# Second norm by its weights alone, the row applied to up's results, one more column pair by seven products, and down's first operands loaded earlier

## The chip, the cores and the metric

The kernel runs on one core of one Trainium2 chip. The metric is the device time of one execution in microseconds; of several runs the median is given.

## The reference

Two layers of an encoder work on 1024 prompt frames and 8 x 16 new frames of running streams, 1152 columns in all, with 1024 features. In each layer one input projection feeds three kinds of attention heads, an output projection adds their result to x, and an MLP with 4096 inner features follows. The change lies in the MLP:

```python
def _rmsnorm(x, g):
    x32 = x.astype(f32)
    y = x32 * lax.rsqrt(jnp.mean(x32 * x32, axis=-1, keepdims=True) + EPS)
    return (y * g.astype(f32)).astype(x.dtype)

def _mlp(h, w_up, w_down):
    return jnp.square(jax.nn.relu(h @ w_up)) @ w_down
...
        xp = xp + _merge(o_mla, o_gla, g_out, o_ca, gla_out_norm[l], w_out[l])
        xp = xp + _mlp(_rmsnorm(xp, norm2[l]), w_up[l], w_down[l])
```

Per frame the norm is one factor r = rsqrt(mean(x^2) + eps) times a weight per feature. Since r is positive and the same for all features of a frame, relu(r z)^2 = (relu(z) r)^2, and (relu(z) r)^2 needs r only after the product with w_up.

## The kernel before

Features lie on the 128 partitions, frames along the free axis: x is 8 tiles of 128 x 1152 (`xs`), worked on in three groups of G = 384 columns (`gsl(g)`). All products are done with float32 operands split in a high part, rounded to the format of the matmul, and the low rest; each product is three matmuls (high x high, high x low, low x high). `wsplit` and `w_pair` split weights (copy on ScalarE, subtraction on VectorE), `hpc` gives the tiles for split activations from one tag of 48 buffers in turn, `piece` the passing float32 tiles from a tag of 8.

The order on each engine is not written out: the framework orders instructions by a simulated time line, with the order of the program as priority; `tc.high_priority(offset=...)` lifts a block. All transfers go through one queue, that of SyncE, in that order.

The MLP of a layer runs so:

- **Norm** (`norm_group`, `inv_rms`): for each group, squares and sums of the 8 tiles on ScalarE, VectorE and GpSimd; a matmul with ones sums over partitions (tile `ms`), a few small operations make r (`rr`), and matmuls spread it to all partitions (`rb`). Then for each of the 8 tiles VectorE makes x * weight * r (`hf`), ScalarE the high part (`hH`), and VectorE or GpSimd the low part (`hL`). The row r of groups 0 and 1 is kept in `rs`. x goes to memory as `xmid`.
- **Up**: w_up has 32 column blocks, taken in 16 pairs. `up_plain(i, gs)` multiplies pair i for the groups gs. `up_seven(i, rest)` does groups 0 and 1 of a pair as a 2 x 2 block product (two column blocks, two halves of the features, two groups) with seven products instead of eight; it needs sums and differences of blocks of weights (`ws`, split to `wus`) and of activations (`ts`). With rest true it multiplies group 2 plainly (`third`). The sums of activations are made once per layer by `t_prep(j)`, j = 0..3, which loads x again from `xmid` (tile `f`, 4 buffers), multiplies it with weights and r, and forms four sums, each split in two. Pairs 0, 1 and 2 are plain, pairs 3 to 15 go by seven products, of which 3 to 12 with group 2; group 2 of pairs 13, 14, 15 follows plainly at the end.
- **put_u** turns a result z into u = relu(z)^2 and stores it to memory: ScalarE relu and a GpSimd multiplication, or for two of the results of a seven-product pair one VectorE operation. Its tile `u` has 5 buffers, shared with the loads `ur` below.
- **Down**: 8 blocks b of 4 tiles of u. `load_u(b)` loads the 12 pieces of a block, splits them to `uH` and `uL`, and `down_block` multiplies them with w_down (`wdn`) and adds to x; block 0 takes x from `xmid`.

PSUM is given out by `banks`: 6 banks for results (`d`) and 2 for the norm during the norm and pair 0, then 8 for results. `w_raw` loads a block of weights into one of 2 buffers (`wr`).

Of the kernel before, what the change touches and what calls it, by code (L numbers as in the profile page):

```python
# [9 lines left out]
F32 = mybir.dt.float32  # L10
F32R = mybir.dt.float32r
U32 = mybir.dt.uint32
AF = mybir.ActivationFunctionType
ALU = mybir.AluOpType
AX = mybir.AxisListType

P = 128
# [4 lines left out]
G = 384  # L22
NG = NT // G
KD = 8
# [16 lines left out]
def body(ctx, tc, t):  # L41
# [5 lines left out]
    V, S, T, GP = nc.vector, nc.scalar, nc.tensor, nc.gpsimd  # L47
# [3 lines left out]
    def nm(s):  # L51
        uid[0] += 1
        return f"{s}_{uid[0]}"
# [19 lines left out]
    def load(dst, src):  # L73
        nc.sync.dma_start(dst, src)  # L74
# [4 lines left out]
    def open_pool(stack, s, side="left"):  # L79
        return stack.enter_context(tc.tile_pool(name=nm(s), bufs=1, reuse_waits="tile", side=side))  # L80
# [5 lines left out]
    def hpc(s, dt=F32R):  # L86
        return hpool.tile([P, G], dt, tag="h", name=nm(s), bufs=48)
# [5 lines left out]
    def piece(s, shape=None, dt=F32):  # L93
        return ppool.tile(list(shape) if shape else [P, G], dt, tag="p", name=nm(s))
# [42 lines left out]
    def sub_l(eng, lo, src, h):  # L137
        eng.tensor_tensor(lo, src, h.bitcast(F32), ALU.subtract)  # L138
# [14 lines left out]
    def copy(o, i, scale=1.0):  # L153
        S.activation(o, i, AF.Copy, scale=scale)  # L154

    def gsl(g):
        return slice(g * G, (g + 1) * G)
# [41 lines left out]
    def norm_group(xs, gains, hs, g, pool=SQ_POOL):  # L199
        r = inv_rms([x[:, gsl(g)] for x in xs], 1024.0, pool=pool)  # L200
        for c in range(KD):
            hs[c].append((hpc("hH"), hpc("hL")))
            f = piece("hf")
            V.scalar_tensor_tensor(f, xs[c][:, gsl(g)], gains[:, c:c + 1], r, ALU.mult, ALU.mult)  # L204
            copy(hs[c][g][0], f)
            sub_l(V if c % 2 else GP, hs[c][g][1], f, hs[c][g][0])
        return r

    def new_h():
        return [[] for _ in range(KD)]  # L210
# [15 lines left out]
    xs = [xpool.tile([P, NT], F32, name=nm("x")) for _ in range(KD)]  # L226
# [23 lines left out]
    for l in range(DEPTH):  # L250
# [88 lines left out]
        hs = new_h()  # L339
# [876 lines left out]
        xs = [xpool.tile([P, NT], F32, name=nm("x")) for _ in range(KD)]  # L1216
# [30 lines left out]
        ustack, tstack = ExitStack(), ExitStack()  # L1247
        up = open_pool(ustack, "up")
        wextra[0], wturn[0] = up, 0
        gains = sml[:, SM_N2:SM_N2 + 8]  # L1250
        hs = new_h()
        rs = []
        for g in range(NG):
            with tc.high_priority(offset=100):
                r = norm_group(xs, gains, hs, g)
                if g < 2:
                    rs.append(up.tile([P, G], F32, name=nm("rs")))
                    copy(rs[g], r)
                for c in range(KD):
                    store(t["xmid"][:, c, gsl(g)], xs[c][:, gsl(g)])  # L1260
        xstack.close()
        tpool = open_pool(tstack, "tsum", "right")
        ts = [[] for _ in range(5)]

        def u_tile(s):
            return up.tile([P, G], F32, tag="u", name=nm(s), bufs=5)

        def t_prep(j):
            fs = []
            for c in (j, j + KH):  # L1270
                for g in range(2):
                    f = tpool.tile([P, G], F32, tag="f", name=nm("f"), bufs=4)
                    load(f, t["xmid"][:, c, gsl(g)])
                    V.scalar_tensor_tensor(f, f, gains[:, c:c + 1], rs[g], ALU.mult, ALU.mult)
                    fs.append(f)
            f11, f12, f21, f22 = fs
            t1, t2, t3, t4 = (piece("t") for _ in range(4))
            V.tensor_tensor(t1, f12, f11, ALU.subtract)
            V.tensor_tensor(t2, f22, t1, ALU.subtract)
            V.tensor_tensor(t4, f21, t2, ALU.subtract)  # L1280
            GP.tensor_tensor(t3, f22, f12, ALU.subtract)
            for n, f in ((2, t2), (3, t3), (1, t1), (4, t4)):
                o = tuple(tpool.tile([P, G], F32R, name=nm("ts")) for _ in range(2))
                copy(o[0], f)
                sub_l(V, o[1], f, o[0])
                ts[n].append(o)
# [11 lines left out]
            load(raw, src)  # L1298
            return raw

        def put_u(ci, g, z, eng):

            u = u_tile("u")
            if eng is None:
                V.scalar_tensor_tensor(u, z, 0.0, z, ALU.max, ALU.mult)
            else:
                r = piece("r")
                S.activation(r, z, AF.Relu)  # L1308
                eng.tensor_tensor(u, r, r, ALU.mult)  # L1309
            store(t["u"][l, ci, :, gsl(g)], u)  # L1310

        def up_plain(i, gs):
            w = [w_pair(w_raw(t["w_up"][l, 2 * i + c]), "wup") for c in range(2)]
            for g in gs:
                for c in range(2):
                    o = bank("d", "z")[:, :G]
                    dense(o, w[c], lambda k: hs[k][g], KD)
                    put_u(2 * i + c, g, o, GP)

        def up_seven(i, rest):  # L1320
            raw = [w_raw(t["w_up"][l, 2 * i + c]) for c in range(2)]
            a11, a12, a21, a22 = (raw[x][:, y * KH:(y + 1) * KH, :] for x in range(2) for y in range(2))
            sa, sb = (tpool.tile([P, KD, P], F32, tag="ws", name=nm("ws"), bufs=2) for _ in range(2))
            s2, s3, s1, s4 = sa[:, :KH], sa[:, KH:], sb[:, :KH], sb[:, KH:]
            GP.tensor_tensor(s1, a21, a22, ALU.add)
            GP.tensor_tensor(s3, a11, a21, ALU.subtract)
            V.tensor_tensor(s2, s1, a11, ALU.subtract)
            V.tensor_tensor(s4, a12, s2, ALU.subtract)

            def prod(o, w, half, x, first):  # L1330
                for j in range(KH):
                    for k, (wi, ri) in enumerate(((0, 0), (0, 1), (1, 0))):
                        mm(o, w[wi][:, half * KH + j, :], x[j][ri], start=first and j == k == 0,
                           stop=j == KH - 1 and k == 2, skip_group_check=True)

            def third(w, c):
                if rest:
                    o = bank("d", "z")[:, :G]
                    dense(o, w, lambda k: hs[k][2], KD)
                    put_u(2 * i + c, 2, o, GP)  # L1340

            def add(s, o, e):
                z = piece(s)
                V.tensor_tensor(z, o, e, ALU.add)
                return z

            h1 = [[hs[j][g] for j in range(KH)] for g in range(2)]
            h2 = [[hs[j + KH][g] for j in range(KH)] for g in range(2)]
            X, Y, W, Z = (bank("d", "z")[:, :G] for _ in range(4))
            w = w_pair(raw[0], "wup")  # L1350
            prod(X, w, 0, h1[0], True)
            ea = ppool.tile([P, G], F32, tag="q", name=nm("ea"), bufs=4)
            copy(ea, X)
            third(w, 0)
            prod(X, w, 1, h2[0], False)
            put_u(2 * i, 0, X, GP)
            w = w_pair(sa, "wus")
            prod(Y, w, 0, ts[2], True)
            eb = add("eb", Y, ea)
            prod(W, w, 1, ts[3], True)  # L1360
            ec = add("ec", W, eb)
            ws = w_pair(sb, "wus")
            prod(Z, ws, 0, ts[1], True)
            put_u(2 * i + 1, 1, add("z22", Z, ec), None)
            w = w_pair(raw[1], "wup")
            third(w, 1)
            prod(W, w, 1, ts[4], False)
            put_u(2 * i + 1, 0, add("z21", W, eb), None)
            prod(Z, ws, 1, h2[1], False)
            put_u(2 * i, 1, add("z12", Z, eb), GP)  # L1370

        up_plain(0, range(NG))
        banks(d=8)
# [2 lines left out]
        up_plain(1, range(NG))  # L1376
        t_prep(2)
        t_prep(3)
        up_plain(2, range(NG))
        for i in range(3, 16):  # L1380
            up_seven(i, i < 13)
        for i in range(13, 16):
            up_plain(i, (2,))
        tstack.close()


# [1 line left out]
        xpool = open_pool(xstack, "x", "right")  # L1388
        xs = [xpool.tile([P, NT], F32, name=nm("x")) for _ in range(KD)]

        def load_u(b):
            us = []
            for q in range(4):
                row = []
                for g in range(NG):
                    r = u_tile("ur")
                    load(r, t["u"][l, 4 * b + q, :, gsl(g)])
                    o = hpc("uH"), hpc("uL")
                    copy(o[0], r)
                    sub_l(V, o[1], r, o[0])  # L1400
                    row.append(o)
                us.append(row)
            return us

        def down_block(us, b, gs):
            for m in range(KD):
# [12 lines left out]
                    V.tensor_tensor(x, o, x if xo is None else xo, ALU.add)  # L1419

        for b in range(8):
            us = load_u(b)
            if b == 7:
                banks(d=6, nm=2)
            for gs in ((range(NG),) if b < 7 else ((0,), (1,), (2,))):
                down_block(us, b, gs)
# [134 lines left out]
```

## Time and profile before

| | us |
|---|---|
| median of 3 runs | 3238.74 |
| lowest, highest run | 3233.21, 3239.31 |
| profiled execution, its own time | 3230.82 |
| its span, first to last instruction | 3229.0 |
| mean granted TensorE clock | 0.976 of full |
| busy: TensorE, VectorE, ScalarE, GpSimd | 3053.8, 1947.0, 1319.7, 987.2 |
| MLP of layer 0, from the last output projection to its end | about 790 to 1600 |
| MLP of layer 1 | about 2390 to 3210 |

Engines in the profile: PE is TensorE's matmul, PEld its weight load, DVE VectorE, ACT ScalarE, POOL GpSimd, SPq the queue of SyncE that issues transfers. A line of a group or of a tile names the line of the code (often a helper's: L56 is every matmul, L138 every subtraction of a high part, L154 every copy), the tiles as out<-in, sizes and count. In a timeline the first two numbers are start and length in us, and in brackets stands how long the engine was idle before and what ended that. A granted clock of 1.00 is full speed.

### The profile page before, as it was taken

The page shows a single profiled execution, that of the slowest core. Times are in us where ns is not written, and L with a number is a line of the kernel's source. Part 1 is how long each engine was busy: PE and PEld are TensorE (multiplying, and loading weights), DVE is VectorE, ACT ScalarE, POOL GpSimd, SP SyncE. Part 2 cuts the span into 40 slices and gives each one's busy share as a digit, 9 for nine tenths or more (in the row PEclk, how much of TensorE's full clock was granted, in tenths as well). Part 3 has the DMA queues.
Part 4 walks back from the last instruction along what each step waited for, and adds up shares of the span by engine and source line. Part 5 has one row for each costly group of instructions (what it writes and reads, how often), then busy time and mean ns, then how long its engine had stood idle before and what let it go on. Part 6 is the DMA issues. An engine that isn't in the chain of part 4 may idle for free.

```text
span 3229.0 us, 50225 instructions
## 1 busy us (share of the span) xinstructions
PE 3053.8 (95%) x18196; PEld 2920.9 (90%) x18196; DVE 1947.0 (60%) x3805; ACT 1319.7 (41%) x2907; POOL 987.2 (31%) x1170
## 2 busy tenths in 40 slices
PE   7999998998999989999999999988999999899998
PEld 7888887887999989999989898878889999899998
DVE  4665597885844555444556646968857444554446
ACT  4554454774322232212345534557743222322213
POOL 4332356552533320000143313655534233200002
PEclk9999999999999999999999999999999999999999
DMA  5333215225322345322343322142353222543223
GB/s 178 113 100 102 91 50 163 77 81 180 117 96 93 102 154 182 99 71 90 115 149 121 101 82 86 63 145 78 109 168 105 97 99 98 183 144 98 92 70 118
DMA packets 221719, 360.20 MB, mean 112 GB/s; under 512 B 27136, under 2 KB 185568, under 8 KB 221472
## 3 DMA queue, kind: packets, MB, share of 16 engines
q1 hardware_dynamic: 221472, 357.00, 34.5%
q8 instruction: 144, 2.36, 0.3%
q14 instruction: 103, 0.84, 0.1%
HBM read 253.87 MB, written 103.02 MB: 111 GB/s over the span
## 4 chain that ended last, share of the span: by engine, by line
PE 74%; DVE 12%; ACT 5%; DMA 4%; issue 3%; POOL 1%; SPq 1%; DVEq 0%; ACTq 0%; POOLq 0%
PE z L56 62%; PE pv L56 3%; PE s L56 2%; PE ptp L71 2%; DMA wr<-in_w_up_dram 1%; DVE hf L204 1%; SPq L74 1%; ACT P L419 1%; DMA cf<-zs_dram 1%; PE glao L56 1%; DVE ng L414 1%; PE rb L56 1%; DVE sbd L825 1%; DVE mq L763 1%; DVE ga L772 1%
## 5 line engine op out<-in xcount | busy, mean ns | idle before, releaser
L56 PE MATMUL z<-uH,wdn 128*128 128x384 f32 x3072 | 786.4, 336 | 10.3 <-ACT uH L154 10.3
L56 PEld LDWEIGHTS z<-uH,wdn 128*128 128x128 f32 x3072 | 558.2, 189 | 11.5 <-ACT uH L154 11.5
L56 PE MATMUL z<-uL,wdn 128*128 128x384 f32 x1536 | 515.0, 336 | 0.0
L56 PE MATMUL z<-hH,wup 128*128 128x384 f32 x1824 | 472.9, 334 | 1.0 <-ACT r L1308 1.0
L1419 DVE TENSOR_TENSOR x<-z,x 128x384 f32<-128x384 f32 x336 | 186.7, 556 | 311.7 <-PE z L56 310.6
L56 PEld LDWEIGHTS z<-hH,wup 128*128 128x128 f32 x1824 | 330.2, 188 | 1.6 <-ACT r L1308 1.6
L56 PE MATMUL z<-hL,wup 128*128 128x384 f32 x912 | 306.6, 336 | 8.5 <-DVE hL L138 7.8
L56 PEld LDWEIGHTS z<-uL,wdn 128*128 128x128 f32 x1536 | 290.0, 189 | 0.0
L1309 POOL TENSOR_TENSOR u<-r 128x384 f32<-128x384 f32 x140 | 163.5, 1172 | 373.7 <-ACT r L1308 263.5
L169 POOL TENSOR_TENSOR sq<-x 128x384 f32<-128x384 f32 x28 | 26.4, 944 | 813.5 <-DVE x L1419 742.0
L1292 ACT ACTIVATE wdn<-wr 128x1024 fp32r<-128x1024 f32 x80 | 84.7, 1059 | 461.0 <-PE z L56 459.9
L138 DVE TENSOR_TENSOR wup<-wr,wup 128x1024 fp32r<-128x1024 f32 x76 | 96.4, 1268 | 203.4 <-ACT wup L1292 203.2
L419 ACT ACTIVATE P<-s,ng 128x320 f32<-128x320 f32 (+5 forms) x288 | 157.7, 552 | 96.4 <-DVE ng L416 61.9
L56 PEld LDWEIGHTS z<-hL,wup 128*128 128x128 f32 x912 | 171.2, 188 | 12.1 <-DVE hL L138 10.8
L56 PE MATMUL z<-ts,wus 128*128 128x384 f32 x936 | 171.7, 340 | 6.5 <-ACT wus L1292 5.9
L138 DVE TENSOR_TENSOR PT<-ptp,PT 128x512 fp32r<-128x512 f32 (+3 forms) x288 | 146.4, 515 | 51.7 <-ACT PT L154 43.7
L154 ACT ACTIVATE PT<-ptp 128x512 fp32r<-128x512 f32 (+3 forms) x288 | 128.4, 460 | 116.6 <-PE ptp L71 115.3
L56 PEld LDWEIGHTS z<-ts,wus 128*128 128x128 f32 x936 | 165.3, 191 | 9.0 <-ACT wus L1292 7.8
L71 PE MATMUL ptp<-ident,P 128*128 128x128 f32 x792 | 138.8, 280 | 20.0 <-DVE PT L138 8.0
L414 DVE TENSOR_REDUCE ng<-s 128x1 f32<-128x320 f32 (+5 forms) x288 | 146.6, 515 | 7.1 <-PE s L56 3.8
L154 ACT ACTIVATE uH<-ur 128x384 fp32r<-128x384 f32 x192 | 98.1, 524 | 126.3 <-PE z L56 79.1
L1308 ACT ACTIVATE r<-z 128x384 f32<-128x384 f32 x140 | 67.8, 487 | 193.3 <-PE z L56 192.2
(439 smaller groups left out, 7267.9 us busy)
## 6 DMA issues: line engine op xcount, KB each, us to landing
wr<-in_w_down_dram SPq DMA_DIRECT2D x80, 512.0 KB, 3.3
wr<-in_w_up_dram SPq DMA_DIRECT2D x76, 512.0 KB, 3.7
u_dram<-u SPq DMA_DIRECT2D x192, 192.0 KB, 2.1
ur<-u_dram SPq DMA_DIRECT2D x192, 192.0 KB, 3.1
zs_dram<-z SPq DMA_DIRECT2D x102, 192.0 KB, 1.9
wo1r<-in_w_out_dram SPq DMA_DIRECT2D x48, 320.0 KB, 3.0
cf<-zs_dram SPq DMA_DIRECT2D x144, 96.0 KB, 2.6
of<-os_dram SPq DMA_DIRECT2D x48, 192.0 KB, 3.2
```

Of the source, the lines that this page charges most:

```text
L56: i = T.matmul(*a, **k).ins
L71: T.transpose(out, in_, idn)
L74: nc.sync.dma_start(dst, src)
L138: eng.tensor_tensor(lo, src, h.bitcast(F32), ALU.subtract)
L154: S.activation(o, i, AF.Copy, scale=scale)
L204: V.scalar_tensor_tensor(f, xs[c][:, gsl(g)], gains[:, c:c + 1], r, ALU.mult, ALU.mult)
L414: V.tensor_reduce(ng[:, x:x + 1], sc[x][:, :hi - lo], AX.X, ALU.max, negate=True)
L419: S.activation(pr[:, lo:hi], sc[x][:, :hi - lo], AF.Exp, bias=ng[:, 0:1], accum_out=ss[:, x:x + 1])
L1292: S.activation(h, raw, AF.Copy)
L1308: S.activation(r, z, AF.Relu)
L1309: eng.tensor_tensor(u, r, r, ALU.mult)
L1419: V.tensor_tensor(x, o, x if xo is None else xo, ALU.add)
```

## The change

- `raw_group` takes the place of `norm_group` in the MLP: the operands of up are x times the weights alone. ScalarE makes the high part with the weight as scale, VectorE the low part from x in one operation. r is computed by `inv_rms` and kept in `rs` for all three groups.
- `put_u` multiplies relu(z) with r on VectorE and squares the result in place on ScalarE, for all results.
- `t_prep` scales the loaded x with the weight alone, on ScalarE.
- Pairs 0 and 1 are plain, 2 to 15 go by seven products, 2 to 13 of them with group 2; group 2 of pairs 14 and 15 follows plainly.
- `load_u` moves ahead of the last stage: the first block's loads stand in the program between the plain products of pairs 14 and 15, with buffers of the tag that `t_prep` loads into. The loads of the later blocks get a pool `dn` of their own with 6 buffers.

```diff
--- before.py
+++ after.py
@@ -205,6 +205,14 @@
             copy(hs[c][g][0], f)
             sub_l(V if c % 2 else GP, hs[c][g][1], f, hs[c][g][0])
         return r
+
+    def raw_group(xs, gains, hs, g):
+
+        for c in range(KD):
+            hs[c].append((hpc("hH"), hpc("hL")))
+            x = xs[c][:, gsl(g)]
+            copy(hs[c][g][0], x, scale=gains[:, c:c + 1])
+            V.scalar_tensor_tensor(hs[c][g][1], x, gains[:, c:c + 1], hs[c][g][0].bitcast(F32), ALU.mult, ALU.subtract)
 
     def new_h():
         return [[] for _ in range(KD)]
@@ -1252,10 +1260,9 @@
         rs = []
         for g in range(NG):
             with tc.high_priority(offset=100):
-                r = norm_group(xs, gains, hs, g)
-                if g < 2:
-                    rs.append(up.tile([P, G], F32, name=nm("rs")))
-                    copy(rs[g], r)
+                raw_group(xs, gains, hs, g)
+                rs.append(up.tile([P, G], F32, name=nm("rs")))
+                copy(rs[g], inv_rms([x[:, gsl(g)] for x in xs], 1024.0))
                 for c in range(KD):
                     store(t["xmid"][:, c, gsl(g)], xs[c][:, gsl(g)])
         xstack.close()
@@ -1271,7 +1278,7 @@
                 for g in range(2):
                     f = tpool.tile([P, G], F32, tag="f", name=nm("f"), bufs=4)
                     load(f, t["xmid"][:, c, gsl(g)])
-                    V.scalar_tensor_tensor(f, f, gains[:, c:c + 1], rs[g], ALU.mult, ALU.mult)
+                    copy(f, f, scale=gains[:, c:c + 1])
                     fs.append(f)
             f11, f12, f21, f22 = fs
             t1, t2, t3, t4 = (piece("t") for _ in range(4))
@@ -1298,15 +1305,11 @@
             load(raw, src)
             return raw
 
-        def put_u(ci, g, z, eng):
+        def put_u(ci, g, z):
 
             u = u_tile("u")
-            if eng is None:
-                V.scalar_tensor_tensor(u, z, 0.0, z, ALU.max, ALU.mult)
-            else:
-                r = piece("r")
-                S.activation(r, z, AF.Relu)
-                eng.tensor_tensor(u, r, r, ALU.mult)
+            V.scalar_tensor_tensor(u, z, 0.0, rs[g], ALU.max, ALU.mult)
+            S.activation(u, u, AF.Square)
             store(t["u"][l, ci, :, gsl(g)], u)
 
         def up_plain(i, gs):
@@ -1315,7 +1318,7 @@
                 for c in range(2):
                     o = bank("d", "z")[:, :G]
                     dense(o, w[c], lambda k: hs[k][g], KD)
-                    put_u(2 * i + c, g, o, GP)
+                    put_u(2 * i + c, g, o)
 
         def up_seven(i, rest):
             raw = [w_raw(t["w_up"][l, 2 * i + c]) for c in range(2)]
@@ -1337,7 +1340,7 @@
                 if rest:
                     o = bank("d", "z")[:, :G]
                     dense(o, w, lambda k: hs[k][2], KD)
-                    put_u(2 * i + c, 2, o, GP)
+                    put_u(2 * i + c, 2, o)
 
             def add(s, o, e):
                 z = piece(s)
@@ -1353,7 +1356,7 @@
             copy(ea, X)
             third(w, 0)
             prod(X, w, 1, h2[0], False)
-            put_u(2 * i, 0, X, GP)
+            put_u(2 * i, 0, X)
             w = w_pair(sa, "wus")
             prod(Y, w, 0, ts[2], True)
             eb = add("eb", Y, ea)
@@ -1361,13 +1364,27 @@
             ec = add("ec", W, eb)
             ws = w_pair(sb, "wus")
             prod(Z, ws, 0, ts[1], True)
-            put_u(2 * i + 1, 1, add("z22", Z, ec), None)
+            put_u(2 * i + 1, 1, add("z22", Z, ec))
             w = w_pair(raw[1], "wup")
             third(w, 1)
             prod(W, w, 1, ts[4], False)
-            put_u(2 * i + 1, 0, add("z21", W, eb), None)
+            put_u(2 * i + 1, 0, add("z21", W, eb))
             prod(Z, ws, 1, h2[1], False)
-            put_u(2 * i, 1, add("z12", Z, eb), GP)
+            put_u(2 * i, 1, add("z12", Z, eb))
+
+        def load_u(b, pool, n):
+            us = []
+            for q in range(4):
+                row = []
+                for g in range(NG):
+                    r = pool.tile([P, G], F32, tag="f", name=nm("ur"), bufs=n)
+                    load(r, t["u"][l, 4 * b + q, :, gsl(g)])
+                    o = hpc("uH"), hpc("uL")
+                    copy(o[0], r)
+                    sub_l(V, o[1], r, o[0])
+                    row.append(o)
+                us.append(row)
+            return us
 
         up_plain(0, range(NG))
         banks(d=8)
@@ -1376,11 +1393,11 @@
         up_plain(1, range(NG))
         t_prep(2)
         t_prep(3)
-        up_plain(2, range(NG))
-        for i in range(3, 16):
-            up_seven(i, i < 13)
-        for i in range(13, 16):
-            up_plain(i, (2,))
+        for i in range(2, 16):
+            up_seven(i, i < 14)
+        up_plain(14, (2,))
+        us = load_u(0, tpool, 4)
+        up_plain(15, (2,))
         tstack.close()
 
 
@@ -1388,19 +1405,7 @@
         xpool = open_pool(xstack, "x", "right")
         xs = [xpool.tile([P, NT], F32, name=nm("x")) for _ in range(KD)]
 
-        def load_u(b):
-            us = []
-            for q in range(4):
-                row = []
-                for g in range(NG):
-                    r = u_tile("ur")
-                    load(r, t["u"][l, 4 * b + q, :, gsl(g)])
-                    o = hpc("uH"), hpc("uL")
-                    copy(o[0], r)
-                    sub_l(V, o[1], r, o[0])
-                    row.append(o)
-                us.append(row)
-            return us
+        dn = open_pool(ustack, "dn")
 
         def down_block(us, b, gs):
             for m in range(KD):
@@ -1419,7 +1424,8 @@
                     V.tensor_tensor(x, o, x if xo is None else xo, ALU.add)
 
         for b in range(8):
-            us = load_u(b)
+            if b:
+                us = load_u(b, dn, 6)
             if b == 7:
                 banks(d=6, nm=2)
             for gs in ((range(NG),) if b < 7 else ((0,), (1,), (2,))):
```

## The prediction

> **What bounds the kernel now.** I read the page first (busy shares, clock row, chain), then the busy times of TensorE by stretches of time through the two MLPs, then the waits inside the stretches that are not full, then the durations of the operations that the change swaps.
>
> ```profile
> PE 3053.8 (95%) x18196; PEld 2920.9 (90%) x18196; DVE 1947.0 (60%) x3805; ACT 1319.7 (41%) x2907; POOL 987.2 (31%) x1170
> ...
> PE 74%; DVE 12%; ACT 5%; DMA 4%; issue 3%; POOL 1%; SPq 1%; DVEq 0%; ACTq 0%; POOLq 0%
> ```
>
> TensorE is 95% busy and holds 74% of the chain; a gain must take matmuls away or close a gap of TensorE. The next rows are stretches of time (start:end in us, length, busy us and count of each engine, granted clock, DMA share, GB/s): layer 0, then the same stages of layer 1.
>
> ```profile
> 820.00:850.00 30.00, 25.59 (x149) 23.99 (x149) 24.18 (x40) 13.62 (x29) 17.84 (x15) 1.00 0.18 59
> 850.00:900.00 50.00, 50.00 (x291) 50.00 (x290) 36.51 (x45) 16.53 (x33) 22.43 (x19) 1.00 0.42 137
> 1138.00:1170.00 32.00, 28.15 (x149) 26.59 (x148) 22.17 (x26) 10.58 (x14) 11.92 (x9) 0.95 0.36 115
> 1200.00:1215.00 15.00, 9.93 (x40) 9.28 (x39) 5.20 (x7) 4.87 (x10) 2.87 (x2) 0.77 0.90 299
> 1215.00:1300.00 85.00, 85.00 (x493) 85.00 (x492) 44.70 (x79) 22.59 (x38) 0.00 (x0) 1.00 0.48 158
> 2420.00:2450.00 30.00, 25.61 (x149) 24.01 (x148) 24.19 (x39) 13.50 (x29) 17.42 (x15) 1.00 0.18 57
> 2738.00:2770.00 32.00, 27.88 (x150) 26.32 (x149) 21.90 (x26) 10.59 (x15) 12.13 (x9) 0.97 0.36 116
> 2800.00:2815.00 15.00, 9.77 (x42) 9.22 (x41) 5.25 (x8) 6.15 (x11) 2.87 (x2) 0.80 0.88 292
> ```
>
> Full stretches give the pace: 493 matmuls in 85 us, 0.1724 us each (the 336 ns that a group shows per matmul overlap two by two). Against this pace three stretches of each layer fall short: the second norm (idle 30 - 25.59 = 4.4 us, clock full), the end of up (149 matmuls where 32/0.1724 = 186 fit: 37 x 0.1724 = 6.3 us, in layer 1 6.1), and the passage from up to down (40 where 87 fit: 8.1 us, in layer 1 7.8). Between them, from 850 to 1600 us, matmuls follow one another without a gap. What ended the idle times, from TensorE's timeline, and the clock behind two of them:
>
> ```profile
> 829.39 0.44 PE L56 MATMUL z<-hL,wup 128*128 128x384 f32 x1 [1.09 <-DVE hL L138]
> 841.20 0.44 PE L56 MATMUL z<-hL,wup 128*128 128x384 f32 x1 [1.89 <-DVE hL L138]
> 1139.19 2.33 PE L56 MATMUL z<-ts,wup 128*128 128x384 f32 x12 [0.74 <-DVE ec L1344]
> 1146.92 5.06 PE L56 MATMUL z<-ts,wus 128*128 128x384 f32 x26 [1.24 <-ACT wus L1292]
> 1165.74 0.96 PE L56 MATMUL z<-ts,wus 128*128 128x384 f32 x4 [1.58 <-ACT wus L1292]
> 1167.00 5.30 PE L56 MATMUL z<-ts,wus 128*128 128x384 f32 x20 [0.29 <-DVE wus L138]
> 1208.58 1.31 PE L56 MATMUL z<-uH,wdn 128*128 128x384 f32 x2 [5.07 <-ACT uH L154]
> ...
> 1166.00:1170.00 4.00, 3.71 (x14) 3.38 (x14) 3.86 (x3) 2.37 (x4) 2.35 (x2) 0.64 0.52 180
> ...
> 1208.00:1212.00 4.00, 3.42 (x10) 3.09 (x11) 2.19 (x4) 2.08 (x4) 0.00 (x0) 0.51 0.99 332
> 1212.00:1216.00 4.00, 4.00 (x17) 4.00 (x16) 1.18 (x3) 1.70 (x4) 0.00 (x0) 0.64 0.92 289
> ```
>
> The 5.07 us wait at the start of down is followed by about 7 us of slow clock: 10 matmuls where 20 fit in the 3.4 busy us, 17 where 23 fit, so 16 x 0.1724 = 2.8 us more; 5.07 + 2.8 = 7.9, which agrees with the 8.1 by count. The second wait for the combined weights (1.58 + 0.29) is followed by a clock of 0.64: 14 matmuls where some 22 fit, 1.4 us more.
>
> **One column pair more by seven products.** A plain pair computes columns 0 and 1 with 2 x 2 x 8 x 3 = 96 matmuls, a seven-product pair with 7 x 4 x 3 = 84; group 2 costs 48 in both. Pair 2 moves over: 12 x 0.1724 = 2.07 us per layer, 4.1 in all. With it come 4 combinations of weights and two more splits per layer on POOL, DVE and ACT, and one pair of weight loads and its splits less, since group 2 of pair 13 no longer loads its weights again. DVE was 36.5 of 50 us and ACT 16.5 busy in 850 to 900, so this lies beside TensorE: nothing.
>
> **One seven-product pair fewer without group 2.** Three such pairs follow one another before, two after; the two waits for combined weights (1146.92 and 1165.74) lie at the two passages between them, where only 48 matmuls (8.3 us) stand between the release of the raw weights and the next need of their sums. One passage goes. If what stays is the cheap one, 1.58 + 0.29 + 1.4 = 3.3 us are saved; if the dear one, 1.24. The column results now pass DVE twice more there (2 x 0.6 us beside 22.17 of 32), which may lengthen the remaining one by up to 0.6. I take 2.0; the ends are 0.6 and 3.3.
>
> On the clock a page and the rows differ: the Trainium skill ("TensorE: Matmul & The Clock Gate", section on HAM oscillation) has it that the clock falls only behind idle gaps of more than about 3.4 us. By it the passage would cost 1.87 us at most instead of 3.3; the sum below would be 1.4 us per layer smaller at its upper end and the same at the value taken. The row of 1166 to 1170, with 0.64 behind two short gaps, is against it.
>
> **The raw norm.** Operands of up no longer wait for the mean square: what was DVE multiply, ACT copy, DVE or POOL subtract behind the row r is ACT copy with a scale and DVE multiply-subtract behind x.
>
> ```profile
> L204 DVE SCALAR_TENSOR_TENSOR hf<-x,smalls,rb x96: 600/606/615, 18.2 to 2439.8; 128x384 f32<-128x384 f32 x96
> L154 ACT ACTIVATE hH<-hf x96: 506/525/536, 18.8 to 2442.1; 128x384 fp32r<-128x384 f32 x96
> L138 POOL TENSOR_TENSOR hL<-hf,hH x48: 992/1023/3412, 20.2 to 2443.4; 128x384 fp32r<-128x384 f32 x48
> L138 DVE TENSOR_TENSOR hL<-hf,hH x48: 542/552/1371, 22.4 to 2445.0; 128x384 fp32r<-128x384 f32 x48
> L1305 DVE SCALAR_TENSOR_TENSOR u<-z x52: 544/557/1201, 916.7 to 2777.8; 128x384 f32<-128x384 f32 x52
> L1308 ACT ACTIVATE r<-z x140: 466/492/527, 838.0 to 2805.1; 128x384 f32<-128x384 f32 x140
> L1309 POOL TENSOR_TENSOR u<-r x140: 822/1143/1808, 839.0 to 2805.7; 128x384 f32<-128x384 f32 x140
> L171 ACT ACTIVATE sq<-x x92: 504/524/528, 3.3 to 3217.6; 128x384 f32<-128x384 f32 x92
> L419 ACT ACTIVATE P<-s,ng 128x384 f32<-128x384 f32 x48 | 27.7, 579 | 18.4 <-DVE ng L414 15.0 <-DVE ng L416 2.8
> ```
>
> Per group of columns DVE gives up 8 x 0.606 and 4 x 0.552 and takes 8 x about 0.606: 2.2 us less; POOL loses 4 x 1.0. ACT's 8 copies stay; a scale held in a tile may cost some 0.05 each more (an estimate: 579 ns of the activation with a per-row operand against 525), off the path. x of group 2 is there at about 817 us, eight copies and eight subtractions take some 5 us side by side, and group 2 is needed only 96 matmuls (16.6 us) after up begins. So the chain of squares, sums, row and broadcast leaves the path, and what ends last is TensorE's own queue, which still holds the sums and broadcasts in between: a late one stops it. Ends 1.0 (these keep most of it) and 4.4; I take 3.6 per layer.
>
> **The row at up's results.** Each of the 96 results per layer is now one DVE multiply (0.56 to 0.61) and one ACT square (0.52) in place. Before, 70 went ACT 0.49 then POOL 1.14, and 26 through DVE alone. Over the layer DVE gets 70 x 0.6 + 26 x 0.05 = 43 us more in some 390 us in which it was about half busy, ACT 96 x 0.52 - 70 x 0.49 = 16, POOL loses 80. A bank of PSUM comes free 0.1 us later, hidden by eight banks. The square waits on ACT for DVE, and the weight copies queued behind it wait too; a seven-product pair with group 2 lasts 132 x 0.1724 = 22.8 us against under 14 us of DVE, so the cover is wide: nothing. rs must be there before the first multiply; with six banks in this phase it has 6 x 24 x 0.1724 = 24.8 us before TensorE stops.
>
> **Sums of x made from raw loads.** 16 multiplies per layer go from DVE (0.607) to ACT (0.52 to 0.58), and no longer need rs. The first seven-product pair, however, now comes a plain pair earlier, and needs all these sums.
>
> ```profile
> 817.91 1.29 SPq L74 DMA_DIRECT2D f<-xmid_dram  x1
> 839.80 0.32 SPq L77 DMA_DIRECT2D u_dram<-u  x1
> 840.17 1.38 SPq L74 DMA_DIRECT2D f<-xmid_dram  x3
> ...
> 843.27 1.37 DVE L1274 SCALAR_TENSOR_TENSOR f<-f,smalls,rs 128x384 f32<-128x384 f32 x1
> 889.07 2.11 DVE L138 TENSOR_TENSOR ts<-t,ts 128x384 fp32r<-128x384 f32 x3
> 907.27 5.01 PE L56 MATMUL z<-ts,wus 128*128 128x384 f32 x28
> ```
>
> Before, they take 843.3 to 891.2 (47.9 us) and are needed at 907.3. After, the need comes at 907.3 - 144 x 0.1724 - 3.6 = 878.9. They can start sooner: the second load stood in SP's queue behind the first store of u (839.80), which the norm held up; that store should now come some 15 to 18 us sooner, so the sums should run from about 826 to 874. I take no stall, with 5 us to spare; the ends are 0 and the case below.
>
> **Down's first operands.** Twelve loads of 192 KB go ahead of pair 15 of the last plain pairs, into four buffers that the sums no longer use, instead of five that the stores of u also used. Their split results take the oldest 24 of 48 slots, all read for the last time by the first 24 matmuls of the last seven-product pair; from there 60 + 96 matmuls (26.9 us) are left before down. At the 299 GB/s of the stretch, 2.36 MB take 7.9 us, and twelve copies and subtractions about 7. So they fit, and the 7.9 us go, unless SP's queue (in order) holds pair 15's two weight loads behind loads that wait for a buffer: some landing of 3.7 us and splitting of 2.3 would then show as up to 6 us. Ends 2 and 7.9; I take 7.0.
>
> ```profile
> wr<-in_w_up_dram SPq DMA_DIRECT2D x76, 512.0 KB, 3.7
> ```
>
> **Sum.** 2.07 + 2.0 + 3.6 + 7.0 = 14.7 us per layer, 29.3 for two. The profiled execution took 3230.82 us (span 3229.0), so it would be 3201.5; it lies 7.9 us below the median of the three runs, 3238.74. Against that median: 3209.4.
>
> **Rivals.** First, slower: the first seven-product pair waits for its sums. If each of the four preparations took the 18.4 us that the third takes here (866.2 to 884.6) and started at 826, they would end at 899.6: 20.7 us late, plus 2.8 of slow clock, 23.5 against 14.7, so 8.8 lost per layer and 3256. It decides from 11.9 us of lateness on (14.7 - 2.8). For it: the third and fourth are placed behind pair 1 in the program. Against it: the 48 us of before hold already such waits, and DVE has less to do.
>
> ```profile
> 866.20 0.60 DVE L1274 SCALAR_TENSOR_TENSOR f<-f,smalls,rs 128x384 f32<-128x384 f32 x1
> ...
> 884.09 0.54 DVE L138 TENSOR_TENSOR ts<-t,ts 128x384 fp32r<-128x384 f32 x1
> ```
>
> Second: the loads for down do not get ahead, because SP's queue keeps them where they were or they push pair 15's weights: 7.0 falls to 1 or so, 17 us less gain altogether, 3226. Third: the row's own matmuls in TensorE's queue keep the norm's stalls (3.6 to 1.0) and the dear passage stays (2.0 to 0.6): 8 us less, 3217.
>
> **How the numbers follow.** Likeliest, all four as taken: 0.55. The third rival 0.14, the second 0.16, the first or a milder wait of its kind 0.15, of which 0.07 lie within 0.2% of before (3232.3 to 3245.2, about what a measurement of this kernel can tell) and 0.05 above; the upper end of the second adds 0.02 and 0.01. All bounds at their good end, 2 x (2.07 + 3.3 + 4.4 + 7.9) = 35.3, give 3203; with some 5 us for the spread of the runs (3233 to 3239) the range begins at 3197. It ends at 3234, taking in the second rival and half a stall at the first pair. The likeliest alone has 3201 to 3216. Faster 0.85, same 0.09, slower 0.06.
>
> **What would show it.** Right: no wait of TensorE for hL behind the second norm; a first pair whose matmuls on ts follow without a gap, and ts done before; one wait for wus at the end of up instead of two; down's first matmul right behind the last of up, with the clock at 1.00 there; POOL nearly empty through up. Wrong: a wait of TensorE for ts at about 875 us, for wup before the last plain pair, for a broadcast or sum of the norm, or a stretch of clock near 0.5 anywhere in the MLP.

## The result, and the profile after

The changed kernel takes 3211.82 us (median of 6 runs, 3202.21 to 3213.99), the kernel before 3235.97 us (6 runs, 3224.92 to 3239.62): a ratio of 0.9916 with a 95% interval of 0.9900 to 0.9933. Forecast were 3209.4 us, between 3197 and 3234. The total came out nearly as forecast, but several of its terms did not. One execution of a variant below, load_shared, took 4254.3 us at a granted clock of 0.649 and is left out of that variant's ratio.

From the page of the changed kernel, busy shares and the chain by engine:

```profile
PE 3041.5 (95%) x18172; PEld 2911.2 (91%) x18172; DVE 1974.7 (62%) x3903; ACT 1371.0 (43%) x2995; POOL 811.4 (25%) x1010
...
PE 74%; DVE 11%; ACT 5%; DMA 4%; issue 3%; POOL 1%; SPq 1%; DVEq 0%; ACTq 0%; POOLq 0%
```

TensorE has 24 matmuls less (18172 for 18196), as the product with seven parts says. GpSimd lost 176 us, VectorE and ScalarE took 28 and 51. None of that says where 28.6 us of span went, so the two MLPs are cut into stages at four events that both kernels have: the first matmul of the last attention product (tile `mso`), the first matmul on the sums of x (`ts`), the first of down (`uH`), the last of down. One row per stage: the first three stages of layer 0 and the first two of layer 1 (columns as in the prediction). Before:

```profile
783.25:907.27 124.02, 116.83 (x682) 113.11 (x683) 85.52 (x131) 46.47 (x96) 58.56 (x51) 1.00 0.42 141
907.27:1208.58 301.31, 292.39 (x1669) 290.50 (x1668) 146.88 (x174) 89.54 (x122) 93.24 (x75) 0.99 0.34 113
1208.58:1614.68 406.10, 406.10 (x2335) 405.77 (x2336) 206.14 (x348) 99.79 (x161) 12.65 (x11) 0.99 0.35 113
2384.47:2507.73 123.26, 116.30 (x681) 113.16 (x682) 86.40 (x131) 46.28 (x96) 58.45 (x51) 1.00 0.44 142
2507.73:2809.47 301.74, 292.39 (x1669) 290.51 (x1668) 147.38 (x174) 89.70 (x123) 91.91 (x75) 0.99 0.34 113
```

After:

```profile
786.69:887.83 101.14, 93.68 (x538) 91.26 (x539) 68.49 (x118) 52.98 (x109) 25.51 (x20) 0.97 0.52 166
887.83:1203.61 315.78, 313.84 (x1802) 311.87 (x1802) 185.61 (x250) 115.06 (x169) 37.87 (x26) 1.00 0.35 115
1203.61:1606.54 402.93, 402.93 (x2336) 402.93 (x2336) 200.01 (x334) 93.22 (x146) 12.66 (x11) 1.00 0.33 107
2367.21:2467.52 100.31, 92.35 (x538) 89.83 (x538) 68.13 (x118) 52.63 (x109) 24.88 (x20) 0.98 0.52 168
2467.52:2782.81 315.29, 313.58 (x1801) 312.01 (x1801) 185.67 (x251) 115.53 (x169) 38.37 (x26) 1.00 0.35 116
```

The full pace stands in one stretch of the second stage without idle time:

```profile
900.00:1130.00 230.00, 230.00 (x1328) 230.00 (x1327) 129.72 (x172) 78.71 (x112) 29.36 (x20) 1.00 0.30 100
```

1328 matmuls in 230 us are 0.1732 us each. Read with it, per layer:

- First stage, norm and the plain pairs: 144 matmuls fewer are 24.9 us, but the stage is only 22.9 us shorter. Net of its work it got 2 us longer. Its idle time is as before (7.5 for 7.2 us) and its clock fell from 1.00 to 0.97.
- Second stage, seven products to down: 133 matmuls more are 23.0 us (132 and 22.9 in layer 1), and it grew by 14.5 (13.6 in layer 1). Idle plus slow clock fell by 8.5 and 9.3 us.
- Down: the same matmuls in 3.2 us less, the slow clock of its first microseconds.

From start to end of the two MLPs that is 24.1 us of 1663. The other 4.5 us of the span's difference lie outside the MLPs. In the attention stage of layer 0, which has the same order of instructions in both kernels, the changed kernel was 3.4 us slower (783.25 to 786.69); in that of layer 1 it was 9.1 us faster, and behind the last MLP 1.1 us slower. Over the runs below, the first mark of layer 0 moves between 782.8 and 794.1 us for instructions in one and the same order, and when one and the same kernel was profiled twice, the attention stage of layer 1 took 760.7 and 767.6 us. So stages are compared here, not spans.

The waits that were to go, in TensorE's timeline of the changed kernel:

```profile
853.04 0.69 PE L56 MATMUL z<-hH,wup 128*128 128x384 f32 x1 [2.63 <-DVE u L1311]
...
1165.54 2.31 PE L56 MATMUL z<-ts,wup 128*128 128x384 f32 x12 [0.74 <-DVE ec L1347]
1173.16 3.56 PE L56 MATMUL z<-ts,wus 128*128 128x384 f32 x19 [0.39 <-ACT wus L1299]
1190.99 0.44 PE L56 MATMUL z<-hH,wup 128*128 128x384 f32 x1 [0.59 <-ACT wup L1299]
1203.61 0.33 PE L56 MATMUL z<-uH,wdn 128*128 128x384 f32 x1
```

The 5.07 us ahead of down are gone (the last row has no bracket: no wait), one passage with 0.39 us is left of two with 1.24 and 1.87, and no wait for `hL` stands behind the norm. In its place is a new one, 2.63 us for a multiply of a result, with this clock behind it (and 2.83 us in layer 1):

```profile
850.00:854.00 4.00, 1.37 (x6) 1.05 (x5) 3.77 (x6) 3.79 (x8) 1.37 (x1) 0.83 0.38 115
854.00:858.00 4.00, 4.00 (x19) 4.00 (x18) 3.14 (x7) 2.44 (x5) 0.57 (x1) 0.74 0.90 260
```

VectorE's timeline there shows why:

```profile
846.47 0.55 DVE L1311 SCALAR_TENSOR_TENSOR u<-z,rs 128x384 f32<-128x384 f32 x1
846.93 0.55 DVE L138 TENSOR_TENSOR ts<-t,ts 128x384 fp32r<-128x384 f32 x1
848.67 0.56 DVE L1285 TENSOR_TENSOR t<-f,f 128x384 f32<-128x384 f32 x1 [1.18 <-ACT f L154]
850.23 0.56 DVE L1286 TENSOR_TENSOR t<-f,t 128x384 f32<-128x384 f32 x1 [1.00 <-ACT f L154]
850.70 1.35 DVE L138 TENSOR_TENSOR ts<-t,ts 128x384 fp32r<-128x384 f32 x1
851.98 0.55 DVE L1287 TENSOR_TENSOR t<-f,t 128x384 f32<-128x384 f32 x1
852.45 0.54 DVE L1311 SCALAR_TENSOR_TENSOR u<-z,rs 128x384 f32<-128x384 f32 x1
```

VectorE stands idle twice for loaded x that ScalarE scales, with the multiply of pair 0's fifth result (the last row) queued behind. That result had been complete since 846.25 us and its row r since 844.6, so the multiply waited only for its turn. TensorE had finished the six results of pair 0 and could not begin pair 1 until that bank was free.

### The profile page after: what moved, and what is told of

Its sections match the earlier page's. It is cut to its first block, busy times and chain, and to the rows that moved or that the text cites. A ratio compares the mean times of both kernels' runs of the same rounds, so it can differ in the third digit from the quotient of the medians.

```text
span 3200.4 us, 50248 instructions
## 1 busy us (share of the span) xinstructions
PE 3041.5 (95%) x18172; PEld 2911.2 (91%) x18172; DVE 1974.7 (62%) x3903; ACT 1371.0 (43%) x2995; POOL 811.4 (25%) x1010
## 4 chain that ended last, share of the span: by engine, by line
PE 74%; DVE 11%; ACT 5%; DMA 4%; issue 3%; POOL 1%; SPq 1%; DVEq 0%; ACTq 0%; POOLq 0%
PE z L56 61%; PE pv L56 3%; PE s L56 2%; PE ptp L71 2%; DMA wr<-in_w_up_dram 1%; DMA cf<-zs_dram 1%; ACT P L427 1%; PE lev L56 1%; PE glao L56 1%; DVE ng L422 1%; SPq L74 1%; DVE ga L780 1%; PE rb L56 1%; DVE sbd L833 1%; DVE mq L771 1%
## 5 line engine op out<-in xcount | busy, mean ns | idle before, releaser
L56 PE MATMUL z<-hH,wup 128*128 128x384 f32 x1728 | 451.8, 336 | 6.9 <-DVE u L1311 5.5
L1424 DVE TENSOR_TENSOR x<-z,x 128x384 f32<-128x384 f32 x336 | 186.9, 556 | 315.8 <-PE z L56 314.5
L56 PEld LDWEIGHTS z<-hH,wup 128*128 128x128 f32 x1728 | 314.7, 189 | 9.1 <-DVE u L1311 6.1
L56 PE MATMUL z<-hL,wup 128*128 128x384 f32 x864 | 290.4, 336 | 0.0
L1312 ACT ACTIVATE u<-u 128x384 f32<-128x384 f32 x192 | 100.0, 521 | 280.3 <-DVE u L1311 276.3
L1311 DVE SCALAR_TENSOR_TENSOR u<-z,rs 128x384 f32<-128x384 f32 x192 | 106.5, 555 | 156.9 <-PE z L56 155.0
L427 ACT ACTIVATE P<-s,ng 128x320 f32<-128x320 f32 (+5 forms) x288 | 157.7, 552 | 99.9 <-DVE ng L424 63.5
L1328 POOL TENSOR_TENSOR ws<-wr 128x512 f32<-128x512 f32 x28 | 46.3, 1653 | 537.7 <-DMA wr<-in_w_up_dram 440.2
L56 PE MATMUL z<-ts,wus 128*128 128x384 f32 x1008 | 180.5, 335 | 0.8 <-ACT wus L1299 0.8
L56 PEld LDWEIGHTS z<-ts,wus 128*128 128x128 f32 x1008 | 174.9, 188 | 1.6 <-ACT wus L1299 1.4
L56 PEld LDWEIGHTS z<-hL,wup 128*128 128x128 f32 x864 | 163.2, 189 | 0.0
```

The source lines that it names most:

```text
L56: i = T.matmul(*a, **k).ins
L427: S.activation(pr[:, lo:hi], sc[x][:, :hi - lo], AF.Exp, bias=ng[:, 0:1], accum_out=ss[:, x:x + 1])
L1311: V.scalar_tensor_tensor(u, z, 0.0, rs[g], ALU.max, ALU.mult)
L1312: S.activation(u, u, AF.Square)
```

## The experiments

All kernels below were timed against the kernel before. Most differ by less than their intervals can hold apart, so each is also read by the stages of its profiled execution (us; first mark to ts, ts to down, down, for both layers, and the sum over both MLPs; down is counted here to the start of its last matmul, 0.33 us before the end shown above):

| kernel | layer 0 | layer 1 | both MLPs | median, ratio to before (95%) |
|---|---|---|---|---|
| before | 124.0, 301.3, 405.8 | 123.3, 301.7, 407.0 | 1663.1 | 3235.97 |
| changed | 101.1, 315.8, 402.6 | 100.3, 315.3, 403.9 | 1639.1 | 3211.82, 0.9916 (0.9900 to 0.9933) |
| again | 100.2, 316.1, 402.6 | 99.8, 316.1, 403.9 | 1638.7 | 3211.81, 0.9934 (0.9914 to 0.9954) |
| plain3 | 125.1, 292.6, 402.6 | 125.9, 293.0, 403.9 | 1643.1 | 3212.76, 0.9942 (0.9921 to 0.9964) |
| rest13 | 99.9, 319.8, 403.6 | 99.9, 316.3, 404.9 | 1644.4 | 3211.41, 0.9935 (0.9915 to 0.9954) |
| load_late | 100.9, 316.0, 402.6 | 99.9, 315.1, 403.9 | 1638.5 | 3214.62, 0.9942 (0.9923 to 0.9961) |
| load_shared | 99.4, 318.9, 405.6 | 99.6, 319.6, 406.5 | 1649.5 | 3223.48, 0.9960 (0.9942 to 0.9979) |
| oldnorm2 | 101.0, 317.7, 402.6 | 99.9, 319.2, 403.9 | 1644.2 | 3217.48, 0.9937 (0.9921 to 0.9954) |
| rawnorm_only | 124.4, 301.4, 405.6 | 123.5, 296.6, 408.1 | 1659.6 | 3234.74, 0.9994 (0.9981 to 1.0007) |
| order | 96.4, 316.5, 402.6 | 95.5, 316.0, 403.9 | 1630.9 | 3200.82, 0.9902 (0.9883 to 0.9920) |
| order_again | 96.6, 316.5, 402.6 | 95.4, 314.7, 403.9 | 1629.7 | 3201.85, 0.9898 (0.9880 to 0.9917) |
| order_low | 97.6, 316.2, 402.6 | 96.9, 316.1, 403.9 | 1633.3 | 3206.87, 0.9903 (0.9887 to 0.9919) |

plain3, and the kernels with two plain pairs, differ by one plain pair of work between the first two stages; their sums compare directly.

**The changed kernel once more (again).**

> The changed kernel once more, beside the others of this call. Theory: 3212 as before; its profile has the wait of 2.6 to 2.8 us for a multiply of a result in both layers, since that is the order of instructions and not chance. Rival (the wait is chance of one execution): it is missing in one of the layers. The stretches outside the MLP, the same program, may lie some 3 us per layer either way.

Its MLPs are 0.3 us from those of the first execution. The wait is there in both layers, 1.0 and 2.6 us; where it is short, another one some 30 us earlier goes with a slow clock (1.4 us for a broadcast at 823):

```profile
819.00:829.00 10.00, 8.60 (x43) 8.28 (x43) 10.00 (x22) 6.91 (x15) 1.94 (x2) 0.77 0.41 137
```

The wait is the order's; its size is not fixed. The sum repeats within 0.3 us here (1.2 us for order below), a single stage within 0.9 (1.3).

**Down's loads late again, buffers of their own (load_late).**

```diff
         up_plain(14, (2,))
-        us = load_u(0, tpool, 4)
         up_plain(15, (2,))
...
-            if b:
-                us = load_u(b, dn, 6)
+            us = load_u(b, dn, 6)
```

> Undone: the first block's loads for down stand after the last plain pair again, with the six buffers of their own pool. Theory (the loads were late because of their place in the program): the wait of TensorE before down's first matmul comes back with about 5 us and 2.8 us of slow clock behind it, 7.9 us per layer, so 3212 + 16 = 3228. Rival (they were late only because they shared five buffers with the stores of u, and their own buffers would do): no wait before down, 3212. A gap of 1 to 4 us says that both have a part.

No wait for `uH`; the MLPs are as long as in the changed kernel, though waits for wup of 1.8 and 0.9 us stand at the end of up. The place in the program was worth nothing.

**Late again, and in the shared buffers (load_shared).** As load_late, and

```diff
-                    r = pool.tile([P, G], F32, tag="f", name=nm("ur"), bufs=n)
+                    r = u_tile("ur")
```

> As the run before with the loads of down's first block behind the last plain pair, but the loads use the five buffers that they share with the stores of u, as before the change; everything else as changed. Theory (the sharing made down wait): TensorE waits about 5 us before down's first matmul and loses 2.8 us to the slow clock behind it in each layer, 16 us in all, 3228. Rival (what freed the loads is that u is now made in 1.1 us on VectorE and ScalarE instead of 1.6 us with GpSimd, so that even shared buffers come free in time): a wait under 1 us, 3212.

The wait comes back, 10.6 us over both MLPs against the mean of the two executions of the changed kernel. The medians differ by 11.7 us, the ratios to before by 6 to 14. Its waits of TensorE, layer 0 from 1130 and layer 1 from 2730 us (total, times, longest):

```profile
PE z L56 <- ACT uH L154: 4.0, 1, 4.0
...
PE z L56 <- ACT uH L154: 5.4, 2, 5.3
```

and SyncE's queue ahead of it:

```profile
1203.33 0.80 SPq L77 DMA_DIRECT2D u_dram<-u  x2
1204.21 0.41 SPq L74 DMA_DIRECT2D wr<-in_w_down_dram  x1
1204.67 2.05 SPq L74 DMA_DIRECT2D ur<-u_dram  x4
```

The first loads of down are issued only behind the last stores of u, whose buffers they take. Sharing was the cause. The waits (4.0 and 5.4 us) and the longer down (3.0 and 2.6 us) come to 15.0 us, near the 16 expected; the sum over the MLPs is smaller in part because the first stages, which the edit does not touch, came out 1.8 us shorter in this execution.

**Three seven-product pairs without group 2 instead of two (rest13).**

```diff
-            up_seven(i, i < 14)
+            up_seven(i, i < 13)
+        up_plain(13, (2,))
         up_plain(14, (2,))
```

> Same matmuls as the changed kernel, but three seven-product pairs without group 2 (13, 14, 15) and three plain pairs behind them, as before. Theory (each passage between two such pairs costs, and the second one is the dear one): two waits for the combined weights again, 1.2 to 3.3 us more per layer, 3214 to 3218. Rival (the passages were dear because GpSimd multiplied the results of up and kept the sums of weights waiting; with GpSimd free each costs about 0.4 us): two waits of about 0.4 us, 3212 to 3213.

Waits of TensorE, layer 0 from 1140 us, layer 1 from 2720:

```profile
PE z L56 <- ACT wus L1299: 2.6, 2, 2.2
PE z L56 <- DVE wus L138: 1.1, 1, 1.1
...
PE z L56 <- DVE wus L138: 1.1, 1, 1.1
PE z L56 <- ACT wus L1299: 0.6, 1, 0.6
```

The second passage costs again, 5.5 us over both MLPs; GpSimd's leaving did not make it cheap. The medians cannot hold this apart from the changed kernel.

**Before's norm and results with the other parts (oldnorm2).** `norm_group`, `put_u` and the multiply in `t_prep` as before; two plain pairs, loads early.

> The other parts without the raw norm: norm, results of up and sums of x made as before the change, but two plain pairs and the early loads of down. Theory (the raw norm is what lets the first seven-product pair come sooner): the sums of x are ready at about 891 us of before's time and needed at 882, so TensorE waits some 9 us for them and loses 2.8 us to the slow clock, in each layer; 3236 less 2 x (2.1 + 11.4 - 11.5) is 3232. Rival (the order of instructions adapts and the sums come in time): no wait for ts, 3209, and then the raw norm is worth nothing or less.

The theory fell: TensorE does not wait for ts itself. The order adapted: TensorE's first matmul on ts begins at 890.6 us, the last part of the sums is done only at 896.7, and other products fill the time between. The first stage is as long as with the raw norm. TensorE's waits of layer 0, norm and first products, then from 1130 us:

```profile
PE z L56 <- DVE hL L138: 3.9, 4, 1.9
PE z L56 <- DVE ec L1352: 2.0, 1, 2.0
...
PE z L56 <- ACT wus L1300: 1.2, 1, 1.2
```

The norm's stalls are there (3.9), the wait for a bank is not. 5.3 us are lost, all of them behind the first matmul on ts. The longest of these waits, 2.0 us for `ec`, followed back through the queues:

```profile
893.88 0.38 SPq L74 DMA_DIRECT2D wr<-in_w_up_dram  x1
899.60 1.30 POOL L1333 TENSOR_TENSOR ws<-wr 128x512 f32<-128x512 f32 x1 [4.19 <-DMA wr<-in_w_up_dram]
900.94 1.73 DVE L1335 TENSOR_TENSOR ws<-ws,wr 128x512 f32<-128x512 f32 x1 [1.55 <-POOL ws L1333]
902.59 0.55 DVE L1352 TENSOR_TENSOR ec<-z,eb 128x384 f32<-128x384 f32 x1
```

On VectorE `ec` stands behind a difference of weights that waits for GpSimd, and GpSimd was idle until its weights had landed. Their load was issued behind the last loads of x for the late sums (881.6 to 886.1 us) and four early loads of down (890.3 to 893.8 us).

**The raw norm alone on the kernel before (rawnorm_only).** `raw_group`, `put_u`, `t_prep` as changed; three plain pairs, pairs 13 to 15 without group 2, loads in the shared buffers.

> The raw norm, its row at up's results and the sums from raw loads alone, on the kernel before: three plain pairs, three seven-product pairs without group 2, and loads of down in the shared buffers behind the last plain pair. Theory (the wait for a bank behind the sums of x comes from this part alone): a wait of 1 to 3 us for a multiply of a result in both layers, the first stretch of the MLP 2 us per layer longer than before, 3240, or less if the passages or the loads of down gain by GpSimd's leaving. Rival (the wait comes from the earlier first seven-product pair, which presses the sums together): no such wait, the norm gains 3.6 us per layer, 3229.

Alone it cannot be told from no change by the runs (0.9994); by the stages its MLPs are 3.5 us shorter, with down's first wait at 2.8 and 2.6 us in place of 5.1 and 5.2. The wait for a bank is there (0.5 and 2.5 us), with two plain pairs between, so it comes from this part alone, and the stage of the norm is 0.3 us longer than before. Both passages stay dear (waits for wus of 3.8 and 1.9 us), with GpSimd free.

**Three plain pairs (plain3).**

```diff
-        for i in range(2, 16):
+        up_plain(2, range(NG))
+        for i in range(3, 16):
```

> The changed kernel with three plain pairs instead of two (seven products from pair 3 on, two of these pairs without group 2 as changed). Theory (the 12 matmuls per layer are worth their pace, and nothing else hangs on the pair): 2.07 us more per layer, MLP of both layers together 4 us longer than in the changed kernel, 3216. Rival (the earlier first seven-product pair presses the sums of x against pair 0's results and makes the wait for a bank): that wait goes here, some 4 us per layer come back, 3208.

4.2 us over both MLPs, twice 12 matmuls. The wait for a bank stays (2.7 and 4.2 us), so the rival falls.

**VectorE's order fixed (order, order_again).** The names of the multiplies are kept in a list, and the first subtraction of each preparation is placed behind one of them:

```diff
+        pu = []
...
-            V.tensor_tensor(t1, f12, f11, ALU.subtract)
+            i = V.tensor_tensor(t1, f12, f11, ALU.subtract).ins
+            tc.add_manual_dep(i, pu[(1, 3, 5, 5)[j]], NOSYNC, reason="order")
...
-            V.scalar_tensor_tensor(u, z, 0.0, rs[g], ALU.max, ALU.mult)
+            pu.append(V.scalar_tensor_tensor(u, z, 0.0, rs[g], ALU.max, ALU.mult).ins.name)
```

> The changed kernel with a fixed order on VectorE: the first subtraction of each preparation of the sums of x stands behind multiplies of pair 0's results (the 2nd, 4th, 6th, 6th). Theory (the 2.6 to 2.8 us wait of TensorE for a bank is a multiply of a result that stands on VectorE behind preparations which wait for loaded x): the wait and the slow clock behind it go, some 4 us per layer, 3204. Rival one (the multiply waits for the row of group 2, which is itself late): the wait stays, 3212. Rival two (the sums are late now): a wait for ts at the first seven-product pair, 3212 or more.

> The version with the fixed order on VectorE once more, to set it against the changed kernel by more runs. Theory (the wait for a bank and its slow clock are gone, 8 us in the two MLPs): 3201 to 3204, no wait for a multiply of a result. Rival (the first result of 3201 was luck in the stages outside the MLP): 3208 to 3212, with the same MLP as the changed kernel.

No wait for a multiply is left in either layer. The first stage of order, to be read beside the changed kernel's 101.14:

```profile
791.22:887.61 96.39, 92.19 (x538) 89.87 (x539) 66.28 (x118) 53.16 (x109) 24.55 (x20) 0.98 0.54 174
```

The same 538 matmuls with 4.2 us idle for 7.5. Both MLPs are 8.0 and 9.2 us shorter than in the mean of the two executions of the changed kernel, the medians 11 and 10 us. This version is the fastest here.

**The row without raised priority (order_low).** As order, with `inv_rms` outside the block of raised priority.

> The version with the fixed order, and the row of the norm (squares, sums, broadcast) without raised priority, since up's operands no longer need it. Theory (what is left of the norm's stalls are matmuls of sums and broadcasts that stand too early in TensorE's queue, 1.2 to 2.7 us per layer, and slow clock behind them): these waits go, 2 to 6 us in all, 3196. Rival (the row comes too late then and TensorE waits for a bank, whose release needs the row): a wait of several us for a multiply of a result, 3204 or more.

The theory fell. The waits only moved: 2.8 us for a broadcast in layer 0, 1.8 us for a multiply in layer 1; the MLPs are 2.4 to 3.6 us longer than in order.

## Why the prediction was right, point by point

Its total was right, and its signs too except in one term. That the total came so near is in part luck: the raw norm, forecast as a gain, cost time, and the passages and down gave more than forecast. Predicted were 29.3 us for two layers, in the MLPs 24.1 were found. The forecast of 3209.4 also started from 3238.74 us, the median of three runs; from the 3235.97 us of six it would have been 3206.7.

- **Twelve matmuls per pair**: 2.07 us per layer predicted; plain3 has 2.1. Right.
- **The passages**: 2.0 predicted, with 3.3 as the best end. By the timelines 1.24 + 1.87 + 1.4 of slow clock, 4.5 us, became 0.39: about 4 us per layer. The step that was mis-sized is "If what stays is the cheap one, 1.58 + 0.29 + 1.4 = 3.3 us are saved": the one that stayed became cheaper as well. Putting the second passage back costs 4.0 and 1.0 us by the second stage of rest13, 2.7 per layer with the first stage and down.
- **Down's first operands**: 7.0 predicted, 7.9 as the end; 5.07 idle and 3.2 of slow clock went in layer 0, 5.23 and 3.1 in layer 1, so about the good end. The sentence "unless SP's queue (in order) holds pair 15's two weight loads" priced a danger of up to 6 us; the waits for wup there are 0.6 us or less. The step had the cause in two places, loads ahead of pair 15 and buffers of their own; load_late and load_shared show that only the buffers count. Nor did the loads keep their place: eight of the twelve were issued at 856 to 873 us, right behind the results that they read, some 320 us before pair 15. The second rival's 17 us do not follow from its own terms: 7.0 falling to 1 is 12 us for two layers, 3221.
- **The raw norm**: 3.6 us gain per layer predicted, 1.0 as the lower end. The first stage lost 2. This is the step that failed, and it failed in the next one, "the row at up's results ... so the cover is wide: nothing". Its count was of busy time, under 14 us of VectorE in 22.8, and of pairs with seven products; it did not ask what stands ahead of the multiplies on VectorE in the first two pairs. There the preparations of ts stand, and they wait for loads. The row was in time (copied at 825.0 us, the first multiply began at 829.5), but TensorE did not have the 24.8 us that six banks were to give. By the timeline pair 1's first result waited for the multiply of pair 0's fifth result, although the first four had been multiplied by 847.0 us. The program gives the banks out anew behind pair 0 (`banks(d=8)`), which is the likely reason, not tested; so the cover was the sixth result alone, 846.3 to 850.4 us. order shows that the multiplies' place is the cause: with them ahead, the stage gains 3.7 to 4.8 us on the changed kernel and, net of the pair's work, 2.5 to 2.9 on before, not far from the 3.6.
- **Sums of x**: right that they come sooner. The first store of u, behind which all but the first of their loads stand, is issued at 830.67 us for 839.80, 9 us sooner where 15 to 18 were taken. The first subtraction starts at 834.4 (826 predicted), the last part is done at 864.5 (874), and TensorE needs them at 887.8 (878.9). The first rival, a wait for ts, did not come. In oldnorm2, where it had most reason to, the sums did end late, and what showed was the 2.0 us for `ec`.
- **What the raw norm is worth**: without the fixed order it brought not the norm's stalls, as argued, but 5.3 us over both MLPs behind the first matmul on ts (oldnorm2). A part is visible in the waits, 2.0 us for `ec` and 1.2 for `wus` in place of 0.39. For `ec` the rows of oldnorm2 show loads that came late, with GpSimd idle; that GpSimd's multiplications made the wait for `wus` is argued, not shown.

The parts undone one by one cost 4.2 (plain3), 5.5 (rest13), 10.6 (load_shared) and 5.3 us (oldnorm2), 25.6 in all, against 24.2 for all together by the same mean of two executions: nearly independent.

On the clock, the Trainium skill's page "TensorE: Matmul & The Clock Gate" (HAM oscillation) names idle gaps of more than about 3.4 us; this case's trace differs again, with 0.74 behind a gap of 2.63 us and 0.77 around gaps of 1.4 us and less. The measurement decides, but it gives no simple rule in its place: the 4 us behind gaps of 1.24 us (before, 1146.92) and 2.02 us (oldnorm2, 903.19) ran at 1.00.

## What to carry to other kernels

Where an operation frees a bank or a buffer that the bounding engine needs, look at what stands ahead of it in its own engine's queue and whether that waits for a load; busy shares do not show it, and an order fixed by hand cost nothing and gave 8 us. Loads that shared buffers with stores were issued only behind the last stores; buffers of their own were what helped here, and an earlier place in the program was not. When effects are a few microseconds, compare stages between events that both kernels have, since the stages that were not touched move by as much from run to run (7 us between two profiles of one kernel).

## What was not expected of the hardware

The same instructions in the same order took 782.8 to 794.1 us up to the first mark, with no change in the kernel there; the granted clock in those stages lay between 0.88 and 1.00 per 100 us. Idle gaps far shorter than the slow stretch behind them went with a lower clock: in the first execution of order a tenth of the first stage still ran at 0.83 (811 to 821 us), behind waits of 0.6 us.

```profile
811.00:821.00 10.00, 9.38 (x49) 9.29 (x48) 10.00 (x19) 7.66 (x17) 4.31 (x4) 0.83 0.62 230
```

Half of that spread is one drop with no such gap before it. In ten of the twelve executions, all but before and rawnorm_only, the clock fell to 0.50 for some microseconds at about 320 us, which cost 5.7 to 5.8 us each time, and TensorE had not been idle for longer than 0.16 us since 290. The same stretch, first of before, then of the changed kernel:

```profile
316.00:334.00 18.00, 18.00 (x126) 15.94 (x126) 6.36 (x16) 6.40 (x16) 0.90 (x5) 1.00 0.18 51
316.00:334.00 18.00, 18.00 (x88) 15.40 (x88) 4.87 (x13) 4.07 (x11) 0.41 (x2) 0.62 0.06 19
```

What sets it off stays open.
